# Hybrid RWKV-7 / pooling decoder block on one core: the SBUF addresses of the up and down projections' tiles, by order and padding

## The chip, the cores and the metric

The kernel is one program on one core of a Trainium2 chip. The metric is the device time of that core in microseconds (us). Before the change it is 2218.88 us, the median of three runs from 2218.65 to 2220.52.

## What is computed

The block is a decoder layer for one sequence of 512 tokens and 2048 channels in float32: an input projection, an RWKV-7 mixer beside a pooling mixer, an output projection, and a gated MLP with a depthwise convolution of width 3 between up projection and activation. Only the MLP matters here:

```python
def _conv_ffn(h, w_up, conv_w, conv_b, w_down):
    u = h @ w_up                         # 512 x 2048 @ 2048 x 11264
    up = jnp.pad(u, ((0, 0), (CONV_WIDTH - 1, 0), (0, 0)))
    y = conv_b
    for j in range(CONV_WIDTH):
        y = y + conv_w[j] * up[:, j:j + T]
    val, gate = jnp.split(y, 2, axis=-1)
    return (jax.nn.silu(gate) * val) @ w_down   # 512 x 5632 @ 5632 x 2048
```

`D_FF` is 5632, which is 44 tiles of 128 columns for the value and 44 for the gate.

## The kernel before

**How a float32 product is made.** Every operand is split into a high part (a copy rounded to the matmul's number format) and a low part (the rest). `mm3` (lines 129 to 133) makes one product of three matmuls: high weights with high activations (line 131), high weights with low activations (132), low weights with high activations (133). Each matmul record in the profile has a weight load (PEld) beside it: the weights are loaded anew for each of the three. `mm2` (1126 to 1128) does the same work in two matmuls where the activations are only 256 columns wide: the high weights with both parts side by side (512 columns, 1127) and the low weights with the high part (256 columns, 1128).

**The weight split.** `wsplit` (1272 to 1284) takes 128 x 1024 raw weights that a DMA has brought. ScalarE copies the high part (tile `uhi`, line 1279), VectorE subtracts for the low part (tile `ulo`, line 1283). Three pairs of buffers take turns: call 0, 3, 6, ... uses `whi0`/`wlo0` and call 1, 4, 7, ... uses `whi1`/`wlo1`, both in the pool `ea`; call 2, 5, 8, ... uses `whi2`/`wlo2` in the pool `ub`.

**The up projection** (about 824 to 1716 us of the profiled execution) is a blocked (Strassen-like) product: seven products of half size for each of the 44 pairs of a value tile and a gate tile. A **product** (`product`, 1286 to 1292) is one `wsplit` and 8 x 3 = 24 matmuls with 256 moving columns into one PSUM bank. There are 44 x 7 = 308 products, 7392 matmuls. I number them from 0 in their order on TensorE; number n uses weight pair n mod 3. Products 0 to 19 come from `first_two`, which makes the first two of the seven for the first ten pairs while the normalised activations of the second half of the tokens are still being made (`combos`). Product 20 is the first one of the main loop (1420 to 1477); product 22 is the first one on a `t` tile. In the main loop a pair in the later part has this order: `Y11` (tiles y0, y1), then the last product of the pair before on `T4` (t40, t41), then `Y21` (y2, y3), `T1` (t10, t11), `T2` (t20, t21), `Y22` (y220, y221), `T3` (t30, t31). Each of these activation tiles is 128 x 2 x 4 x 256 float32, high and low part, 8192 bytes in each partition. The profile leaves out the digits of tile names, so it writes `y` for Y11, Y21 and Y22, and `t` for T1 to T4. The last pair's products are numbers 300 to 306, and 307 is the last one on T4, which is made among the first products of the down projection.

**The down projection** (to the end) has 16 output tiles, and its 44 input tiles `act` are halved into h = 0 and h = 1. Each output tile and half takes three `wsplit` calls, for 8, 8 and 6 input tiles (`down`, 1499 to 1511): blocks of 24, 24 and 18 matmuls of 512 columns with `mm3`. In `down_half`, which makes the last eight output tiles for each half of the tokens, the blocks have 16, 16 and 12 matmuls of `mm2`. The `act` tiles are put into the up projection's places when these are done with (`ATAGS`, 1382): first y0 to y3, then t10, t11, t20, t21, y220, y221, t30, t31, t40.

**Order of work.** The compiler's scheduler sets the order of the instructions on each engine from their dependencies and from when buffers come free. The weight loads of the main loop are issued from SyncE's queue (`r1`, `w11`, `w12`, `w22`, `r3`) and two accumulating ones from GpSimd's.

**Where the tiles lie.** A pool puts its tiles one behind the other in the order in which their tags are first asked for. Pools on the left side follow each other from low addresses, and a pool on the right side ends at byte 229,344 of each partition. Worked out from the order and the sizes in the code, the byte addresses before are:

| tiles | pool | address mod 512 |
|---|---|---|
| y0 to y3 (Y11, Y21) | rb | 192 |
| t40 / t41 (T4) | ea | 224 / 352 |
| t1., t2., t3., y22. (T1, T2, T3, Y22) | ub | 480 |
| whi0, wlo0, whi1, wlo1 | ea | 256 |
| whi2, wlo2 | ub | 384 |
| the output projection's activations and split weights (earlier stage) | act, wts | 384 and 384 |

A slice for one matmul begins at a multiple of 512 bytes from the start of its weight tile and at a multiple of 1024 bytes from the start of its activation tile, so the class mod 512 holds for all slices of a tile. I write 192/256 for activations at 192 and weights at 256.

Small tiles that nothing reads set these classes: `edge` (32 bytes, lines 1274 to 1275) ahead of `whi0` in `ea` and of `whi2` in `ub`, and `edge2` (96 bytes, 1281 to 1282). The tile `ncw` (528 bytes, line 1358) is the last one of the pool `rb` and holds the negated convolution weights of the gate; `finish_pair` (1369) reads it. `rdiag` (1024 bytes, line 175) is a tile of the same pool that each of the RMS normalisations uses shortly.

Of the kernel before, what the change touches and what calls it, by code (L numbers as in the profile page):

```python
# [9 lines left out]
F32 = mybir.dt.float32  # L10
# [6 lines left out]
P = 128  # L17
T = 512
D = 2048
KT = D // P  # L20
NF = 44
# [6 lines left out]
NSLOT = 10  # L28
# [37 lines left out]
def block_kernel(ctx, tc, a, out, stop=None, dbg=None):  # L66
# [1046 lines left out]
    rb = ctx.enter_context(tc.tile_pool(name="rb", bufs=1, reuse_waits="tile"))  # L1113
# [3 lines left out]
    QW = 4 * P  # L1117
# [17 lines left out]
    def quad(i, name, dt=F32):  # L1135
        return rb.tile([P, 4, T], dt, tag=f"x2_{i}", name=name)
# [38 lines left out]
    for k0 in range(4, KT, 4):  # L1175
# [4 lines left out]
        for f in range(8):  # L1180
            out_block(f, k0)
            if k0 == 8 and f % 2:
                t = quad(f // 2, "x2")
# [10 lines left out]
    def out_half(hf, f):  # L1194
        ps = bank()
        acts = half([pairs[k] for k in range(KT)], hf)
        for k0 in range(0, KT, 4):
            wh, wl = split_weights(load_weights(a["wout"][f, :, k0 * P : k0 * P + WC]))
            for kk in range(4):
                sl = slice(kk * P, (kk + 1) * P)  # L1200
                mm2(ps, wh[:, sl], wl[:, sl], acts[k0 + kk], k0 + kk == 0, k0 + kk == KT - 1)
        out_done(f, [ps[:, 0:HT], ps[:, HT:T]], hf * HT, (hf + 1) * HT)
# [28 lines left out]
    for f in range(8, KT):  # L1231
# [7 lines left out]
                next(steps, None)  # L1239
        out_half(1, f)  # L1240

    ea = ctx.enter_context(tc.tile_pool(name="ea", bufs=1, reuse_waits="tile"))
    hctx.close()
    if stop == "B":
        return
# [6 lines left out]


    ub = ctx.enter_context(tc.tile_pool(name="ub", bufs=1, side="right", reuse_waits="tile"))
    free += [(ub, f"s{i}") for i in range(NSLOT)]

    class Slot:
# [12 lines left out]
    nsplit, lo_of = [0], [None]  # L1270

    def wsplit(src):
        n = src.shape[-1]
        if nsplit[0] in (0, 2):
            (ea, None, ub)[nsplit[0]].tile([P, 8], F32, tag="edge", name="edge")
        pool, tag = ((ea, "0"), (ea, "1"), (ub, "2"))[nsplit[0] % 3]
        nsplit[0] += 1
        hi = pool.tile([P, 2 * QW], F32R, tag="whi" + tag, name="uhi")
        S.copy(hi[:, 0:n], src)  # L1279
        lo = pool.tile([P, 2 * QW], F32R, tag="wlo" + tag, name="ulo")  # L1280
        if nsplit[0] in (2, 3):
            pool.tile([P, 24], F32, tag="edge2", name="edge2")
        lo_of[0] = V.tensor_tensor(lo[:, 0:n], src, hi[:, 0:n].bitcast(F32), op=ALU.subtract)  # L1283
        return hi, lo

    def product(ps, w, Y, start=True):
        wh, wl = wsplit(w)
        for k in range(8):
            sl = slice(k * P, (k + 1) * P)
            y = Y[k // 4]  # L1290
            mm3(ps, wh[:, sl], wl[:, sl], y[:, 0, k % 4, :], y[:, 1, k % 4, :], start=start and k == 0,
                stop=k == 7, more=not start)
# [62 lines left out]
        T4[g] = split4(ea, f"t4{g}", t4[g])  # L1355
    free.append((rb, "acc"))

    ncw = rb.tile([P, 3, NF], F32, tag="ncw", name="ncw")
    V.tensor_scalar(ncw, vec[:, COLS["cw"] : COLS["cw"] + 264].rearrange("p (i g j) -> p i g j", i=3, g=2)[:, :, 1, :],
                    -1.0, None, op0=ALU.mult)  # L1360

# [137 lines left out]
    def down(ps, f, h, acts, blocks=(0, 8, 16)):  # L1499
        for k0 in blocks:  # L1500
            n = min(8, NJ - k0)
            w = down_row()
            nc.sync.dma_start(w[:, 0 : n * P], a["wdn"][f, :, (h * NJ + k0) * P : (h * NJ + k0 + n) * P])
            wh, wl = wsplit(w[:, 0 : n * P])
            for k in range(n):
                sl = slice(k * P, (k + 1) * P)
                x = acts[k0 + k]
                if x.shape[-1] == HT:
                    mm2(ps, wh[:, sl], wl[:, sl], x, k0 + k == 0, k0 + k == NJ - 1)
                else:  # L1510
                    mm3(ps, wh[:, sl], wl[:, sl], x[:, 0, :], x[:, 1, :], start=k0 + k == 0, stop=k0 + k == NJ - 1)
# [73 lines left out]
    for f in range(NWF, KT):  # L1585
        n = f - NWF
# [107 lines left out]
```

## Time and profile before

| | us |
|---|---|
| median of three runs | 2218.88 |
| the profiled execution's own time | 2222.13 |
| its span, first to last instruction | 2220.4 |
| TensorE busy | 2157.1 (97%) |
| TensorE weight loads busy | 1890.5 (85%) |
| VectorE busy | 1617.1 (73%) |
| ScalarE busy | 1019.3 (46%) |
| GpSimd busy | 218.0 (10%) |
| mean granted TensorE clock | 0.994 |

A busy time is the union of an engine's records, and a matmul's record is longer than the distance from its start to the next one's start, because matmuls overlap. The pace of TensorE is therefore read from the start times in the timeline: the start of one product to the start of the next, divided by its number of matmuls.

### The profile page before, as it was taken

Reading aid. Unit: us, or ns where it says so; the run is one execution under the profiler, and the core shown is the slowest. Engines: PE = TensorE matmul, PEld = TensorE weight load, DVE = VectorE, ACT = ScalarE, POOL = GpSimd, SP = SyncE. Lnnn points to the kernel's source line nnn. Section 1 sums busy time; section 2 is a strip of 40 time slices with the busy share of each in tenths; the row PEclk is TensorE's granted clock in tenths of the full one; section 3 lists DMA queues with packets and bytes.
Section 4 is the critical chain, followed back from the end, with each engine's and each line's share of the span. In section 5 each row is a group of like instructions: output and inputs, shape, how many; then the busy total and the mean of one; then the engine's idle time right before and its main releaser. Section 6 shows DMA issues by size and latency. Waiting matters only on the chain.

```text
span 2220.4 us, 42522 instructions
## 1 busy us (share of the span) xinstructions
PE 2157.1 (97%) x17060; PEld 1890.5 (85%) x17060; DVE 1617.1 (73%) x2546; ACT 1019.3 (46%) x1465; POOL 218.0 (10%) x352
## 2 busy tenths in 40 slices
PE   6899999999999999999999999999999999999997
PEld 3677777777778889999999999999999888888886
DVE  7998898888853778888888877777777355253464
ACT  4354444444343466555555555555556322233453
POOL 0002111111100101101100000000000000110000
PEclk9999999999999999999999999999999999999998
DMA  9966665666447667988888777777777577564464
GB/s 392 379 207 201 198 200 172 194 185 189 119 132 253 204 174 252 249 249 243 230 242 247 209 200 197 198 204 203 200 194 240 158 287 252 194 206 117 137 194 144
DMA packets 169992, 468.65 MB, mean 211 GB/s; under 512 B 21361, under 2 KB 29505, under 8 KB 161729
## 3 DMA queue, kind: packets, MB, share of 16 engines
q1 hardware_dynamic: 128866, 364.45, 49.5%
q0 software_dynamic: 24752, 72.91, 15.6%
q10 hardware_dynamic: 16176, 28.58, 4.5%
q8 instruction: 134, 2.20, 0.4%
q14 instruction: 64, 0.52, 0.1%
HBM read 433.86 MB, written 31.99 MB: 210 GB/s over the span
## 4 chain that ended last, share of the span: by engine, by line
PE 85%; DVE 8%; DMA 3%; issue 2%; ACT 2%; POOL 0%; DVEq 0%; SPq 0%; ACTq 0%; POOLq 0%
PE b L131 18%; PE b L132 18%; PE b L133 18%; PE mm L555 11%; PE b L1127 5%; PE b L1128 3%; DVE wa L289 3%; DMA wrow<-wup 1%; DMA wraw<-win 1%; PE pb L957 1%; DVE war L674 1%; DVE wlo L328 1%; PE pa L621 0%; PE pb L997 0%; POOL x L797 0%
## 5 line engine op out<-in xcount | busy, mean ns | idle before, releaser
L132 PE MATMUL b<-t,uhi 128*128 128x256 f32 x1408 | 396.2, 281 | 0.0
L131 PE MATMUL b<-t,uhi 128*128 128x256 f32 x1408 | 396.0, 281 | 0.0
L133 PE MATMUL b<-t,ulo 128*128 128x256 f32 x1408 | 395.4, 281 | 0.0
L131 PE MATMUL b<-y,uhi 128*128 128x256 f32 x1056 | 296.0, 280 | 4.0 <-ACT uhi L1279 4.0
L133 PE MATMUL b<-y,ulo 128*128 128x256 f32 x1056 | 294.5, 279 | 0.7 <-DVE ulo L1283 0.7
L132 PE MATMUL b<-y,uhi 128*128 128x256 f32 x1056 | 295.0, 279 | 0.0
L555 PE MATMUL mm<-ahl,whi 128*128 128x512 f32 x864 | 290.8, 410 | 2.0 <-DVE rk L458 1.4
L1283 DVE TENSOR_TENSOR ulo<-wd,uhi 128x1024 fp32r<-128x1024 f32 (+1 forms) x120 | 136.0, 1134 | 205.7 <-ACT uhi L1279 201.1
L133 PEld LDWEIGHTS b<-t,ulo 128*128 128x128 f32 x1408 | 266.0, 189 | 0.0
L132 PEld LDWEIGHTS b<-t,uhi 128*128 128x128 f32 x1408 | 265.0, 188 | 0.0
L131 PEld LDWEIGHTS b<-t,uhi 128*128 128x128 f32 x1408 | 264.7, 188 | 0.0
L1279 ACT CAST uhi<-wquart 128x1024 fp32r<-128x1024 f32 x156 | 163.9, 1051 | 200.0 <-PE b L132 174.8
L1279 ACT CAST uhi<-wd 128x1024 fp32r<-128x1024 f32 (+1 forms) x120 | 117.2, 978 | 280.9 <-PE b L132 230.2
L1283 DVE TENSOR_TENSOR ulo<-wquart,uhi 128x1024 fp32r<-128x1024 f32 x156 | 190.9, 1224 | 65.2 <-ACT uhi L1279 65.0
L1279 ACT CAST uhi<-r 128x1024 fp32r<-128x1024 f32 x132 | 138.7, 1051 | 155.7 <-PE b L132 155.7
L132 PE MATMUL b<-act,uhi 128*128 128x512 f32 x528 | 208.5, 395 | 0.0
L131 PE MATMUL b<-act,uhi 128*128 128x512 f32 x528 | 208.5, 395 | 0.0
L133 PE MATMUL b<-act,ulo 128*128 128x512 f32 x528 | 207.8, 394 | 0.0
L1283 DVE TENSOR_TENSOR ulo<-r,uhi 128x1024 fp32r<-128x1024 f32 x132 | 161.3, 1222 | 60.9 <-ACT uhi L1279 60.9
L131 PEld LDWEIGHTS b<-y,uhi 128*128 128x128 f32 x1056 | 199.1, 189 | 4.5 <-ACT uhi L1279 4.4
L133 PEld LDWEIGHTS b<-y,ulo 128*128 128x128 f32 x1056 | 199.5, 189 | 1.0 <-DVE ulo L1283 0.9
L132 PEld LDWEIGHTS b<-y,uhi 128*128 128x128 f32 x1056 | 199.2, 189 | 0.1
(312 smaller groups left out, 4294.8 us busy)
## 6 DMA issues: line engine op xcount, KB each, us to landing
wquart<-wup SPq DMA_DIRECT2D x176, 512.0 KB, 4.7
wa<-ada SPq DMA_DIRECT2D x48, 1024.0 KB, 7.0
war<-ada SPq DMA_DIRECT2D x192, 256.0 KB, 4.1
wd<-wdn SPq DMA_DIRECT2D x80, 512.0 KB, 4.1
wraw<-win ACTq DMA_DIRECT2D x105, 256.0 KB, 4.2
wraw<-wout SPq DMA_DIRECT2D x96, 256.0 KB, 3.6
wquart<-wup POOLq DMA_DIRECT2D x44, 512.0 KB, 7.0
r<-wup SPq DMA_DIRECT2D x44, 512.0 KB, 4.5
```

Source lines behind the costliest of these rows:

```text
L131: PE.matmul(ps, wh, xh, start=start, stop=False, skip_group_check=more)
L132: PE.matmul(ps, wh, xl, start=False, stop=False, skip_group_check=more)
L133: return PE.matmul(ps, wl, xh, start=False, stop=stop, skip_group_check=more)
L289: V.scalar_tensor_tensor(wa[n], wa[n], 1.0, cb, op0=ALU.mult, op1=ALU.mult, accum_out=mod[:, j : j + 1])
L328: V.tensor_tensor(lo, raws[n], hi[:, :].bitcast(F32), op=ALU.subtract)
L555: PE.matmul(ps, w[:, sl], x, start=first, stop=k == KT - 1 and i == 2)
L674: V.scalar_tensor_tensor(wa, wa, 1.0, cqs[kq], op0=ALU.mult, op1=ALU.mult, accum_out=modq[:, kq, j : j + 1])
L957: PE.matmul(pt[HS[e], h, c * 2 * L : (c + 1) * 2 * L], nt[HS[e], s, :], rw[HS[e], s, :, :], start=True, stop=True)
L1127: PE.matmul(ps[:, :].rearrange("p (a b) -> p a b", a=2), wh, x, start=start, stop=False)
L1128: PE.matmul(ps[:, 0:HT], wl, x[:, 0, :], start=False, stop=stop)
L1279: S.copy(hi[:, 0:n], src)
L1283: lo_of[0] = V.tensor_tensor(lo[:, 0:n], src, hi[:, 0:n].bitcast(F32), op=ALU.subtract)
```

## The change

The change alters the order in which tags are first asked for, and the padding. A helper `lay` asks for a tile of each tag in a given order as soon as a pool is open; nothing reads or writes these tiles. In `ea` the order becomes t40, t41, 64 bytes of padding, then the weight pairs 0 and 1. In `ub` it becomes the ten slots, the eight activation tiles, 64 bytes, `whi2`, `wlo2`, and 224 bytes at the end. `ncw` loses its own place in `rb` and uses that of `rdiag`; `ea` begins where `ncw` began. The calls for `edge` and `edge2` in `wsplit` go. No instruction is added or removed.

```diff
+    def lay(pool, sizes):
+        for tag, n in sizes:
+            pool.tile([P, n], F32, tag=tag, name="lay")
+
     ea = ctx.enter_context(tc.tile_pool(name="ea", bufs=1, reuse_waits="tile"))
+    lay(ea, [("t40", 4 * T), ("t41", 4 * T), ("edge", 16)])
     hctx.close()
...
     ub = ctx.enter_context(tc.tile_pool(name="ub", bufs=1, side="right", reuse_waits="tile"))
+    lay(ub, [(f"s{i}", T) for i in range(NSLOT)])
+    lay(ub, [(f"{t}{g}", 4 * T) for g in range(2) for t in ("t1", "t2", "t3", "y22")])
+    lay(ub, [("edge", 16), ("whi2", 2 * QW), ("wlo2", 2 * QW), ("edge2", 56)])
...
     def wsplit(src):
         n = src.shape[-1]
-        if nsplit[0] in (0, 2):
-            (ea, None, ub)[nsplit[0]].tile([P, 8], F32, tag="edge", name="edge")
         pool, tag = ((ea, "0"), (ea, "1"), (ub, "2"))[nsplit[0] % 3]
...
-        if nsplit[0] in (2, 3):
-            pool.tile([P, 24], F32, tag="edge2", name="edge2")
...
-    ncw = rb.tile([P, 3, NF], F32, tag="ncw", name="ncw")
+    ncw = rb.tile([P, 3, NF], F32, tag="rdiag", name="ncw")
```

Worked out from the new order: `ea` begins at 101,568 (192 mod 512), t40 and t41 lie at 192, the weight pairs 0 and 1 at 256. `ub` is 94,496 bytes, begins at 134,848 (192 mod 512), its slots and its eight activation tiles lie at 192, and `whi2`, `wlo2` at 256. So all products have 192/256. The place of `whi2` and `wlo2` (220,928 to 229,120) is one that the output projection's split weights had; before, it was one that its activations had.

## The prediction

> **What bounds the kernel now.** I read the page's chain first, then the groups of the up projection's main loop, then the windows by stage, and last the timeline of TensorE alone, for its start times. The page's chain, by engine and by line:
>
> ```profile
> PE 85%; DVE 8%; DMA 3%; issue 2%; ACT 2%; POOL 0%; DVEq 0%; SPq 0%; ACTq 0%; POOLq 0%
> PE b L131 18%; PE b L132 18%; PE b L133 18%; PE mm L555 11%; PE b L1127 5%; PE b L1128 3%; DVE wa L289 3%; DMA wrow<-wup 1%; DMA wraw<-win 1%; PE pb L957 1%; DVE war L674 1%; DVE wlo L328 1%; PE pa L621 0%; PE pb L997 0%; POOL x L797 0%
> ```
>
> More than half of the span hangs on the three matmuls of `mm3`. The next rows are groups between 900 and 1704 us (behind the bar: busy time, mean ns of one, then idle time before them with what ended it), and then windows with busy time and count for TensorE, its weight loads, VectorE, ScalarE and GpSimd, and the granted clock, the DMA share and GB/s:
>
> ```profile
> L132 PE MATMUL b<-t,uhi 128*128 128x256 f32 x1392 | 391.7, 281 | 0.0
> L1283 DVE TENSOR_TENSOR ulo<-wquart,uhi 128x1024 fp32r<-128x1024 f32 x152 | 186.1, 1224 | 65.2 <-ACT uhi L1279 65.0
> L1279 ACT CAST uhi<-wquart 128x1024 fp32r<-128x1024 f32 x152 | 159.7, 1051 | 196.5 <-PE b L132 171.3 <-issue 24.9
> ```
>
> ```profile
> core 0: us, PE busy (x) PEld busy (x) DVE busy (x) ACT busy (x) POOL busy (x), PEclk, DMA share, GB/s
> 885.00:900.00 15.00, 15.00 (x134) 15.00 (x134) 15.00 (x15) 8.66 (x11) 3.49 (x5) 1.00 0.96 272
> 900.00:1100.00 200.00, 200.00 (x1695) 200.00 (x1694) 166.20 (x199) 107.99 (x135) 20.96 (x24) 1.00 0.87 245
> 1720.00:2078.00 358.00, 358.00 (x1542) 289.39 (x1541) 156.26 (x165) 104.61 (x132) 26.15 (x48) 1.00 0.59 194
> 2078.00:2220.00 142.00, 127.44 (x719) 110.28 (x717) 80.93 (x109) 64.49 (x84) 3.13 (x2) 0.95 0.59 172
> ```
>
> TensorE never idles here; VectorE waits for ScalarE's high parts, and ScalarE waits for TensorE to give a weight buffer back. So the weights are split ahead of need, and the stage lasts as long as its matmuls follow each other. Only their pace can shorten it.
>
> That pace isn't the same everywhere. First rows of product 17 and of product 22, with five whole products on y0 and y2 between them:
>
> ```profile
> 886.88 0.28 PE L131 MATMUL b<-y,uhi 128*128 128x256 f32 x1
> ...
> 900.48 0.28 PE L131 MATMUL b<-t,uhi 128*128 128x256 f32 x1
> ```
>
> 13.60 us over 120 matmuls is 113.3 ns each. Now the first rows of products 300 to 306, the last pair in the order that the section on the kernel gives:
>
> ```profile
> 1687.62 0.29 PE L131 MATMUL b<-y,uhi 128*128 128x256 f32 x1
> ...
> 1690.37 0.28 PE L131 MATMUL b<-t,uhi 128*128 128x256 f32 x1
> ...
> 1693.21 0.29 PE L131 MATMUL b<-y,uhi 128*128 128x256 f32 x1
> ...
> 1696.04 0.28 PE L131 MATMUL b<-t,uhi 128*128 128x256 f32 x1
> ...
> 1698.88 0.28 PE L131 MATMUL b<-t,uhi 128*128 128x256 f32 x1
> ...
> 1701.72 0.28 PE L131 MATMUL b<-y,uhi 128*128 128x256 f32 x1
> ...
> 1704.59 0.28 PE L131 MATMUL b<-t,uhi 128*128 128x256 f32 x1
> ```
>
> Per matmul (the distance divided by 24), with the classes of the table of addresses: Y11 at 192/256 takes 114.6 ns, T4 at 224 and 352/256 118.3, Y21 at 192/384 117.9, T1 at 480/256 118.3, T2 at 480/256 118.3, Y22 at 480/384 119.6. Shape, engine load and order of instructions are the same in all of them; the addresses differ. The one product at 192/256 is the fast one, and it is the class that all products get. The reader is to see that the 5 x 44 = 220 products on T1 to T4 and Y22, and the third of the y products that has pair 2, run below a pace that this same kernel already reaches, at full clock, in the window from 885 us.
>
> **The change part by part.** *Up projection.* The rows of products 22 and 306 span 284 products, 6816 matmuls: 1704.59 - 900.48 = 804.11 us, 117.97 ns each. At 113.33 ns they take 772.5 us: **-31.6 us**. Products 306 and 307 follow with 48 matmuls at some 5 ns less: **-0.2**. Products 0 to 21 I cost at nothing: most are on y tiles already, and their length is set by stalls of the norm between them.
>
> The saving lies on TensorE's own path, so nothing hides it. What comes late next is the split: per product VectorE's 1.22 us and ScalarE's 1.05 us, against a product of 2.72 us. VectorE's share goes from 166.20/200 = 83% to 87%, the DMA share from 0.87 to 0.91. Both stay under what the row from 885 us shows (VectorE 100%, DMA 0.96) with TensorE full.
>
> A rule of the Trainium skill speaks against all of this. "SBUF — State Buffer", section "Who interferes with whom", gives TensorE two independent read ports, one for the moving operand and one for the weights, and has it wait on nobody. By it the distance of two addresses costs nothing and this term is 0 instead of -31.6. The six products above disagree with it, 114.6 against 118.3 to 119.6 ns, unless their pace has a cause that only goes along with the addresses; that is the second rival.
>
> *Down projection.* The first rows of the second and third block (y0 to y3 with pairs 0 and 1, 192/256), and of three later blocks (y0 to y3 with pair 2, 192/384; then 480/256, 24 matmuls and the start of the 18):
>
> ```profile
> 1716.04 0.39 PE L131 MATMUL b<-act,uhi 128*128 128x512 f32 x1
> ...
> 1721.64 0.39 PE L131 MATMUL b<-act,uhi 128*128 128x512 f32 x1
> ...
> 1772.04 0.39 PE L131 MATMUL b<-act,uhi 128*128 128x512 f32 x1
> ...
> 1777.54 0.40 PE L131 MATMUL b<-act,uhi 128*128 128x512 f32 x1
> ...
> 1783.13 0.40 PE L131 MATMUL b<-act,uhi 128*128 128x512 f32 x1
> ```
>
> With 512 columns the order turns round: 192/256 takes 5.60/24 = 233.3 ns, 192/384 5.50/24 = 229.2, 480/256 5.59/24 = 232.9. The 192/384 blocks come 12 times in the first half (output tiles 4 to 15), 288 matmuls, and lose 4.1 ns each: 1.2 us. Seven blocks of the second half have that class in half of their matmuls: 84 x 4.1 = 0.3. Sum **+1.5**. Whether 192/256 everywhere holds 233.3 no row shows; its other end is that all 1584 matmuls run at the best 229.2 (1296 x 4.1 = 5.3 us gained). I take +1.5, the rows of the very class. The `mm2` blocks:
>
> ```profile
> 2104.55 0.40 PE L1127 MATMUL b<-act,uhi 128*128 128x512 f32 x1
> ...
> 2107.35 0.40 PE L1127 MATMUL b<-act,uhi 128*128 128x512 f32 x1
> ...
> 2109.48 0.39 PE L1127 MATMUL b<-act,uhi 128*128 128x512 f32 x1
> ```
>
> 16 matmuls, half of them at 192/256, take 175.0 ns each; 12 at 480/256 take 177.5. At most 16 x 12 x 2.5 ns = 0.5 us is there to gain; I take 0.
>
> *The new place of pair 2.* It overlaps weights of the output projection, so the third split has to wait for that projection's last matmul:
>
> ```profile
> 829.50 1.03 ACT L1279 CAST uhi<-wrow 128x1024 fp32r<-128x1024 f32 x1
> ...
> 832.16 0.28 PE L1128 MATMUL b<-ahl,wlo 128*128 128x256 f32 x1
> ...
> 837.65 0.37 PE L131 MATMUL b<-y,uhi 128*128 128x256 f32 x1
> ```
>
> The copy starts 2.9 us later, at 832.4, and with VectorE's 1.22 us the pair is ready at 834.7. Product 2, which needs it, starts at 837.65: cost 0, under cover of products 0 and 1; 2.9 us if that cover goes. Behind the copy on ScalarE stands nothing that starts before 833.5.
>
> *`ncw` in the place of `rdiag`.* Before, it is made long ahead; after, it waits until the second norm's TensorE broadcast has read `rdiag`:
>
> ```profile
> L1359 DVE TENSOR_SCALAR ncw<-vec x1: 284/284/284, 665.8 to 665.8; 128x132 f32<-128x132 f32 x1
> ```
>
> ```profile
> 843.28 0.59 PE L181 MATMUL b<-rdiag,cmat 128*128 128x256 f32 x2
> ```
>
> Its 0.28 us fall into the stretch up to 900 us, where VectorE is the full engine (15.00 of 15.00): **+0.3**. No load is moved past a queue, and the padding itself issues nothing.
>
> Sum: -31.6 - 0.2 + 1.5 + 0.3 = **-30.0 us**. The profiled execution, 2222.13 us (span 2220.4), would take 2192.1. It lies 3.25 us above the median, so the median goes from 2218.88 to **2188.9**.
>
> **The rivals.** *First: the slow rhythm returns in part.* Addresses are not all: the five fast products above hold two with pair 2 (192/384), the class that takes 117.9 ns in product 302. And product 4, at 192/256, runs slowly behind a stall:
>
> ```profile
> 843.83 0.28 PE L132 MATMUL b<-y,uhi 128*128 128x256 f32 x1
> ...
> 846.54 0.28 PE L131 MATMUL b<-y,uhi 128*128 128x256 f32 x1
> ```
>
> 2.71/23 = 117.8 ns. So there seem to be two rhythms, and a disturbance can choose between them. Against a long stay in the slow one speaks product 300, which comes behind a slow product and still averages 114.6. If a third of the loop stays slow, a third of 31.6 is lost: 2199.4.
>
> *Second: no gain.* The rhythm is set by the order of work and kept; everything runs at 117.8 as product 4 did. Saved: 6816 x 0.17 = 1.2 us, against +1.8 elsewhere: 2219.5.
>
> *Third: loads or VectorE take over* in the first twenty turns of the loop (its first 200 us show a DMA share of 0.87). These hold 10 x 7 + 10 x 5 = 120 products; if they keep their pace, 120/284 of 31.6 = 13.4 us are lost: 2202.3. Against it, SyncE's queue waits for free buffers (total, times, longest), so loads have time to spare:
>
> ```profile
> SPq L1430 <- DVE ulo L1283: 102.1, 43, 2.5
> ```
>
> *Fourth, the other side: the denser stream lowers the granted clock* in the whole loop. The last stage shows 0.95. At 113.33/117.97 = 0.96 the gain is gone; at 0.94 a matmul takes 120.6 ns, 6816 x 2.6 = 17.7 us more: about 2238. Against it, the window from 885 us is at this density with a clock of 1.00, and the 0.95 stands where TensorE idles 15 of 142 us.
>
> **How the numbers follow.** Forecast 0.77, the first rival 0.09, the second 0.06, the third 0.05, the fourth 0.03. The forecast's own range goes from 2182 (all of the down projection at its best pace) to 2192 (the third split uncovered). Upwards I reach to the first rival's 2199, and leave out the rest. A measurement tells about 0.2% (4.4 us) from no change, so faster is 0.77 + 0.09 + 0.05 = 0.91, same 0.06, slower 0.03.
>
> **What would show it.** Right: starts 113.3 to 113.5 ns apart in t products as in y products, on every third product too; about 772 us from product 22 to product 306; down blocks of 24 in 5.60 us, those of 1772 us as well; a granted clock of 1.00; no wait of TensorE in the loop. Wrong: t products at 117.8 (the second rival), fast and slow stretches by turns (the first), waits for `uhi` or `ulo` (the third).

## The result, and the profile after

The changed kernel takes 2191.57 us (median of 20 runs), the kernel before 2220.62 us (median of 20 runs beside them). The ratio is 0.9874, 95% interval 0.9859 to 0.9889: some 28 us are saved. The profiled execution took 2191.8 us, with a span of 2190.0 us and a mean granted clock of 0.994. Two of the 20 times, 2219.40 and 2223.24, stand 26 us and more above the other eighteen (2189.1 to 2193.3) at the same granted clock (0.995, where the eighteen have 0.993 to 0.997), and the ratio is one of mean times without the higher of the two; no profile of such an execution was taken, and the experiments show a mechanism of that size.

The chain of the changed kernel, by engine and by line, from its page:

```profile
PE 76%; issue 11%; DVE 8%; DMA 3%; ACT 2%; POOL 1%; POOLq 0%; DVEq 0%; SPq 0%; ACTq 0%
PE b L131 16%; PE b L133 16%; PE b L132 16%; PE mm L555 12%; DVE wa L289 3%; PE b L1127 2%; PE b L1128 1%; PE pb L957 1%; DMA al<-ad 1%; DMA wrow<-wup 1%; DVE ulo L1287 1%; DMA x<-dx 0%; PE pa L621 0%; DVE wlo L328 0%; DVE h L313 0%
```

The three matmuls still carry the end, with 16% each in place of 18%. (The 11% of "issue" is time for which this view found no releaser; TensorE is busy there, as the windows show.) The groups between 900 and 1672 us, and windows as before:

```profile
L132 PE MATMUL b<-t,uhi 128*128 128x256 f32 x1391 | 383.9, 276 | 0.0
L1287 DVE TENSOR_TENSOR ulo<-wquart,uhi 128x1024 fp32r<-128x1024 f32 x152 | 185.5, 1221 | 51.2 <-ACT uhi L1285 51.1
L1285 ACT CAST uhi<-wquart 128x1024 fp32r<-128x1024 f32 x152 | 159.7, 1051 | 173.8 <-PE b L132 149.5 <-ACT yv L1367 22.9
```

```profile
core 0: us, PE busy (x) PEld busy (x) DVE busy (x) ACT busy (x) POOL busy (x), PEclk, DMA share, GB/s
885.00:900.00 15.00, 14.34 (x123) 14.15 (x124) 14.79 (x16) 9.06 (x12) 2.96 (x4) 1.00 0.98 276
900.00:1100.00 200.00, 199.86 (x1764) 199.69 (x1763) 172.45 (x208) 112.18 (x142) 21.89 (x25) 1.00 0.89 252
1690.00:2048.00 358.00, 357.69 (x1533) 287.92 (x1532) 155.66 (x164) 103.43 (x130) 26.24 (x48) 1.00 0.58 192
2048.00:2190.00 142.00, 127.17 (x719) 109.93 (x718) 80.91 (x109) 64.53 (x84) 3.14 (x2) 0.96 0.59 172
```

VectorE still waits for ScalarE's high parts (51.1 us in place of 65.0) and ScalarE for TensorE (149.5 in place of 171.3), so the weights are still split ahead of need. The 200 us from 900 us hold 1764 matmuls where they held 1695, at the same clock. The starts of product 22, of products 300 to 303, and of product 306:

```profile
899.44 0.28 PE L131 MATMUL b<-t,uhi 128*128 128x256 f32 x1
...
1656.00 0.28 PE L131 MATMUL b<-y,uhi 128*128 128x256 f32 x1
...
1658.72 0.28 PE L131 MATMUL b<-t,uhi 128*128 128x256 f32 x1
...
1661.44 0.28 PE L131 MATMUL b<-y,uhi 128*128 128x256 f32 x1
...
1664.16 0.28 PE L131 MATMUL b<-t,uhi 128*128 128x256 f32 x1
...
1672.80 0.39 PE L131 MATMUL b<-t,uhi 128*128 128x256 f32 x1 [0.32 <-ACT cap L1464]
```

The loop takes 773.36 us in place of 804.11. Each of the three products between takes 2.72 us, 113.3 ns per matmul, on y and t tiles alike and with every pair of weights; before they took 114.6, 118.3 and 117.9. Product 306 waited 0.32 us, not for weights but for a copy that reads its PSUM bank (`cap`). The first rows of three blocks in the down projection (output tile 4; the first of them is the class that was quick before):

```profile
1740.53 0.40 PE L131 MATMUL b<-act,uhi 128*128 128x512 f32 x1
...
1746.13 0.40 PE L131 MATMUL b<-act,uhi 128*128 128x512 f32 x1
...
1751.73 0.40 PE L131 MATMUL b<-act,uhi 128*128 128x512 f32 x1
```

Both distances are 5.60 us, 233.3 ns per matmul. Between the two profiled executions the balance is: before product 22 -1.0 us (900.48 to 899.44), the loop -30.75, from product 306 to the end +1.45 (515.77 to 517.22): -30.3.

That leaves one thing of the early products, still in the changed kernel, all at 192/256. The starts of products 5 to 7, and of 8 to 10:

```profile
847.88 0.28 PE L131 MATMUL b<-y,uhi 128*128 128x256 f32 x1
...
850.70 0.28 PE L131 MATMUL b<-y,uhi 128*128 128x256 f32 x1
...
853.53 0.28 PE L131 MATMUL b<-y,uhi 128*128 128x256 f32 x1
...
856.32 0.28 PE L131 MATMUL b<-y,uhi 128*128 128x256 f32 x1
...
859.04 0.28 PE L131 MATMUL b<-y,uhi 128*128 128x256 f32 x1
...
861.76 0.28 PE L131 MATMUL b<-y,uhi 128*128 128x256 f32 x1
```

Products 5 and 6 run at 2.82 and 2.83 us, 117.7 ns; product 7 is disturbed; products 8 and 9 run at 2.72 us. The same classes of addresses and the same shapes have two rhythms, that is, two steady distances from start to start. So the addresses can't be the whole story.

### The profile page after: what moved, and what is told of

It reads as the page before. It is cut to its first block, busy times and chain, and to the rows that moved or that the text cites. A ratio compares the mean times of both kernels' runs of the same rounds, so it can differ in the third digit from the quotient of the medians.

```text
span 2190.0 us, 42524 instructions
## 1 busy us (share of the span) xinstructions
PE 2127.7 (97%) x17060; PEld 1858.0 (85%) x17060; DVE 1613.4 (74%) x2546; ACT 1018.5 (47%) x1465; POOL 218.5 (10%) x352
## 4 chain that ended last, share of the span: by engine, by line
PE 76%; issue 11%; DVE 8%; DMA 3%; ACT 2%; POOL 1%; POOLq 0%; DVEq 0%; SPq 0%; ACTq 0%
PE b L131 16%; PE b L133 16%; PE b L132 16%; PE mm L555 12%; DVE wa L289 3%; PE b L1127 2%; PE b L1128 1%; PE pb L957 1%; DMA al<-ad 1%; DMA wrow<-wup 1%; DVE ulo L1287 1%; DMA x<-dx 0%; PE pa L621 0%; DVE wlo L328 0%; DVE h L313 0%
## 5 line engine op out<-in xcount | busy, mean ns | idle before, releaser
L131 PE MATMUL b<-t,uhi 128*128 128x256 f32 x1408 | 388.8, 276 | 0.5 <-ACT cap L1464 0.3
L132 PE MATMUL b<-t,uhi 128*128 128x256 f32 x1408 | 388.6, 276 | 0.0
L133 PE MATMUL b<-t,ulo 128*128 128x256 f32 x1408 | 388.6, 276 | 0.0
L131 PE MATMUL b<-y,uhi 128*128 128x256 f32 x1056 | 292.2, 277 | 1.2 <-ACT uhi L1285 1.2
L132 PE MATMUL b<-y,uhi 128*128 128x256 f32 x1056 | 291.8, 276 | 0.0
L1287 DVE TENSOR_TENSOR ulo<-wquart,uhi 128x1024 fp32r<-128x1024 f32 x156 | 190.3, 1221 | 51.2 <-ACT uhi L1285 51.1
```

The costliest lines, as they stand in the source:

```text
L131: PE.matmul(ps, wh, xh, start=start, stop=False, skip_group_check=more)
L132: PE.matmul(ps, wh, xl, start=False, stop=False, skip_group_check=more)
L133: return PE.matmul(ps, wl, xh, start=False, stop=stop, skip_group_check=more)
```

## The experiments

**Which distance?** Three theories: A, only weights 64 bytes behind the activations let the 113.3 ns rhythm hold; B, any multiple of 64 bytes does; C, it is enough that all products have one class. Four kernels keep everything of the change (order, `ncw`, activations at 192) and set only the padding, so that the weights lie at distance 0, 32, 128 and 192. The edit for 192 (the others have 0, 8 or 32 in place of 48, and 72, 64 or 40 in place of 24; a pad of 0 is left out):

```diff
-    lay(ea, [("t40", 4 * T), ("t41", 4 * T), ("edge", 16)])
+    lay(ea, [("t40", 4 * T), ("t41", 4 * T), ("edge", 48)])
-    lay(ub, [("edge", 16), ("whi2", 2 * QW), ("wlo2", 2 * QW), ("edge2", 56)])
+    lay(ub, [("edge", 48), ("whi2", 2 * QW), ("wlo2", 2 * QW), ("edge2", 24)])
```

> The changed kernel with all activations at 192 as they are, and all split weights at 192 as well (distance 0 in place of 64), by the padding alone. Theory A (the distance of 64 bytes is what lets the 113.3 ns rhythm hold): the loop from product 22 to product 306 runs at 117.8 to 120 ns, some 803 to 818 us in place of 773.4, and the time is 2220 to 2236 us. Theory B (any multiple of 64 bytes does): 113.4 ns, about 2191. Theory C (what counts is that all products have one class, whichever, so that nothing throws the rhythm out): 113.4 ns, about 2191.

> The same with all split weights at 224 (distance 32). A and B: no fast rhythm, 118 to 120 ns per matmul (T4 at 224/256 and 352/384, which have this distance, showed 118.3 before), 2220 to 2236 us. C: 113.4 ns, about 2191.

> The same with all split weights at 320 (distance 128). A: 117.8 to 120 ns, 2220 to 2236 us. B and C: 113.4 ns, about 2191.

> The same with all split weights at 384 (distance 192, the class of Y11 and Y21 with pair 2 before, which showed 113.3 ns in products 17 and 20 and 117.9 in product 302). A in its strict form: 117.8 ns or a change between both, 2195 to 2222 us. A modulo 128, B and C: 113.4 ns, about 2191. In the down projection the blocks of 512 columns at 192/384 took 229.2 to 229.6 ns before; if that holds for all of them, the down projection gains 1584 x 3.9 = 6 us against the changed kernel.

Measured, one run each (the row for 64 is the median from above). The pace of the loop is the distance from product 22 to product 306 over 6816; the pace of the blocks with 512 columns is their mean distance in the down projection:

| distance | time, us | loop, ns per matmul | 512 columns, ns per matmul |
|---|---|---|---|
| 0 | 2228.59 | 120.0 | 226.7 |
| 32 | 2226.48 | 118.3 | 233.3 |
| 64 (the changed kernel) | 2191.57 | 113.5 | 233.3 |
| 128 | 2226.21 | 118.7 | 232.4 |
| 192 | 2213.72 | 117.8 | 228.9 |

The loop and two blocks of the down projection (24 matmuls to the next start) at distance 0, and the loop at distance 192:

```profile
902.63 0.28 PE L131 MATMUL b<-t,uhi 128*128 128x256 f32 x1
...
1720.55 0.28 PE L131 MATMUL b<-t,uhi 128*128 128x256 f32 x1
...
1786.19 0.39 PE L131 MATMUL b<-act,uhi 128*128 128x512 f32 x1
...
1791.63 0.39 PE L131 MATMUL b<-act,uhi 128*128 128x512 f32 x1
```

```profile
899.66 0.28 PE L131 MATMUL b<-t,uhi 128*128 128x256 f32 x1
...
1702.43 0.28 PE L131 MATMUL b<-t,uhi 128*128 128x256 f32 x1
```

817.92 us at distance 0 and 802.77 at 192, against 773.36. B falls (distances 0, 128 and 192 are slow), and so does C (all of them are uniform). The new order and the place of `ncw` can't be what saves 28 us: four kernels that have both are between 6 us faster and 9 us slower than the kernel before (2219.62 beside them). At distances 0, 32, 128 and 192 none of the products, the early ones included, is quicker than the loop: the shortest take 2.88, 2.84, 2.84 and 2.83 us. Distance 0 was not foreseen in one respect: it is the worst for 256 columns and the best for 512, where a block takes 5.44 us in place of 5.60.

**Distance or place?** The same distance, 32 bytes further up:

```diff
+    rb.tile([P, 8], F32, tag="padr", name="lay")
     steps = first_half()
...
-    lay(ub, [("edge", 16), ("whi2", 2 * QW), ("wlo2", 2 * QW), ("edge2", 56)])
+    lay(ub, [("edge", 16), ("whi2", 2 * QW), ("wlo2", 2 * QW), ("edge2", 48)])
```

(the tag stands in `rb` ahead of y0 to y3 and moves all that follows)

> The changed kernel with 32 bytes of padding ahead of y0 and the rest moved along: all activations at 224, all split weights at 288, distance 64 as before. If the distance alone counts: 113.4 ns, 773 us from product 22 to 306, about 2191.5. If the absolute place of 192/256 counts: 117.8 to 120 ns and 2220 to 2230.

Measured, one run: 2191.65 us. Products 22 and 306:

```profile
899.53 0.28 PE L131 MATMUL b<-t,uhi 128*128 128x256 f32 x1
...
1672.01 0.28 PE L131 MATMUL b<-t,uhi 128*128 128x256 f32 x1
```

772.48 us, 113.33 ns in the loop, without a single slow product. The distance counts; 192 and 256 themselves don't.

**One pair alone.** Only the third pair of weights moved away:

```diff
-    lay(ub, [("edge", 16), ("whi2", 2 * QW), ("wlo2", 2 * QW), ("edge2", 56)])
+    lay(ub, [("edge", 48), ("whi2", 2 * QW), ("wlo2", 2 * QW), ("edge2", 24)])
```

> The changed kernel with only the third pair of split weights moved by padding: whi2 and wlo2 at 384 (distance 192, which ran at 117.8 ns throughout when all pairs had it), pairs 0 and 1 at 256 as they are. If each product takes the pace of its own class: every third product 117.8 ns and the others 113.3 to 114.6, some 115 ns on the mean, 784 us from product 22 to 306, and about 2201 us. Rival, a rhythm once thrown out stays out: all products at 117.8 ns, 803 us, about 2220. Rival, two of three pairs are enough: 773 us, about 2191.

Measured, one run: 2192.38 us. Products 22, 31 to 34 and 306 (32 is on the third pair):

```profile
901.69 0.28 PE L131 MATMUL b<-t,uhi 128*128 128x256 f32 x1
...
926.17 0.28 PE L131 MATMUL b<-y,uhi 128*128 128x256 f32 x1
...
929.59 0.35 PE L131 MATMUL b<-t,uhi 128*128 128x256 f32 x1 [0.39 <-ACT uhi L1285]
...
932.49 0.28 PE L131 MATMUL b<-y,uhi 128*128 128x256 f32 x1
...
935.21 0.28 PE L131 MATMUL b<-t,uhi 128*128 128x256 f32 x1
...
1675.39 0.39 PE L131 MATMUL b<-t,uhi 128*128 128x256 f32 x1 [0.18 <-ACT cap L1464]
```

773.7 us, 113.5 ns in the loop, and apart from product 32, behind the stall, the products on the third pair take 113.3 ns as well, the class that ran at 117.8 when it was alone. The last rival holds: two of three pairs are enough. So with 256 columns a class doesn't have one pace; distances 64 and 192 each ran in two rhythms. With 512 columns it is otherwise: in the first half of this run's down projection the blocks on the third pair take 229.2 ns per matmul and the others 232.9 to 233.5 (the first block, which product 307 interrupts, left out), each close to the pace of its own distance in the table.

**Two rhythms?** One more matmul, into a bank that nobody reads, ahead of 34 products; its width grows by 8 columns with each turn of the loop and begins again at 8 after 256:

```diff
+    kick = [0]
+
     def product(ps, w, Y, start=True):
         wh, wl = wsplit(w)
+        if kick[0]:
+            PE.matmul(bank()[:, 0:kick[0]], wh[:, 0:P], Y[0][:, 0, 0, 0:kick[0]], start=True, stop=True)
+            kick[0] = 0
...
+            kick[0] = 8 * (n + 1) % 256 + 8
             product(pa, w11, Y11)
```

> The changed kernel, with one more matmul in each turn of the main loop that has ten or more as its pair (34 turns), ahead of the product of Y11, of 16 to 256 columns into a bank that nothing reads; the rest of the work is the same. It tests whether there are two rhythms at one and the same class that a disturbance chooses between. If so: behind some of these matmuls the products up to the next one run at 117.8 ns, behind others at 113.3, with nothing in between; the time is about 2195 plus 29.6 us times the slow share, 2195 to 2225. Rival, the slow products early in the stage come from their neighbours' work (norms, their loads): all products stay at 113.4 ns, about 2195.

Measured, one run: 2213.37 us, 116.8 ns on the mean. The starts of the first product of five turns in a row in this run (products 167, 174, 181, 188, 195), each behind an additional matmul:

```profile
1303.71 0.30 PE L131 MATMUL b<-y,uhi 128*128 128x256 f32 x1
...
1322.87 0.29 PE L131 MATMUL b<-y,uhi 128*128 128x256 f32 x1
...
1342.77 0.29 PE L131 MATMUL b<-y,uhi 128*128 128x256 f32 x1
...
1362.67 0.28 PE L131 MATMUL b<-y,uhi 128*128 128x256 f32 x1
...
1381.84 0.28 PE L131 MATMUL b<-y,uhi 128*128 128x256 f32 x1
```

A turn of 168 matmuls takes 19.16, 19.90, 19.90, 19.17 us, and 19.04 would be 168 x 113.3 ns. The slow turns are 0.74 us longer, 4.4 ns per matmul. Every turn behind such a matmul ran wholly at 113.3 or wholly at 117.8, once its first few matmuls were over; the rhythm stayed until the next one. That is the theory of two rhythms. The rival is out: the same products ran at 113.4 ns in the changed kernel and, behind some of these matmuls, at 117.8 ns here, with the same work around them.

**Both distances, by use.** The up projection gets distance 64 and the down projection distance 0, from the same buffers:

```diff
-NSLOT = 10
+NSLOT = 9
...
-    lay(ea, [("t40", 4 * T), ("t41", 4 * T), ("edge", 16)])
+    lay(ea, [("t40", 4 * T), ("t41", 4 * T), ("whi0", 2 * QW + 128), ("wlo0", 2 * QW + 128), ("whi1", 2 * QW + 16)])
-    lay(ub, [("edge", 16), ("whi2", 2 * QW), ("wlo2", 2 * QW), ("edge2", 56)])
+    lay(ub, [("wlo1", 2 * QW + 128), ("whi2", 2 * QW + 128), ("wlo2", 2 * QW + 16), ("edge2", 56)])
-    def wsplit(src):
+    def wsplit(src, at=16):
-        hi = pool.tile([P, 2 * QW], F32R, tag="whi" + tag, name="uhi")
+        hi = pool.tile([P, 2 * QW + 16], F32R, tag="whi" + tag, name="uhi")[:, at : at + 2 * QW]
-        lo = pool.tile([P, 2 * QW], F32R, tag="wlo" + tag, name="ulo")
+        lo = (ea if tag == "0" else ub).tile([P, 2 * QW + 16], F32R, tag="wlo" + tag, name="ulo")[:, at : at + 2 * QW]
...
-            wh, wl = wsplit(w[:, 0 : n * P])
+            wh, wl = wsplit(w[:, 0 : n * P], 0)
```

> Distance 64 for the up projection and distance 0 for the down projection: the tiles of the split weights lie at 192 and are 64 bytes longer, the up projection writes and reads them from byte 64 on, the down projection from byte 0 on; for the room, nine slots in place of ten, and wlo1 in the other pool. Up projection at 113.4 ns as in the changed kernel, down projection at 226.7 ns per matmul of 512 columns as with distance 0 everywhere (1584 x 6.6 = 10.5 us less) and about 1 us less in its last part: about 2180 us. If the pace of the down projection had another cause in that run than the distance, 2191. If nine slots are too few, TensorE waits in the loop and it is over 2191.

Measured: 2210.35 us (2206.76 to 2211.21, five runs), ratio to before 0.9946, 95% interval 0.9933 to 0.996. The forecast of 2180 us fell, and the profile says where. Products 31, 32 and 306 of this run:

```profile
924.10 0.28 PE L131 MATMUL b<-y,uhi 128*128 128x256 f32 x1
...
927.38 0.36 PE L131 MATMUL b<-t,uhi 128*128 128x256 f32 x1 [0.39 <-ACT uhi L1285]
...
1701.96 0.28 PE L131 MATMUL b<-t,uhi 128*128 128x256 f32 x1
```

Up to product 31 the loop runs at 113.3 ns. Product 32 waits for its weights for 0.39 us; from there to product 306 it is 774.58 us over 274 x 24 matmuls, 117.8 ns, to the end of the stage. The down projection gained as expected (226.7 ns). One stall of 0.4 us cost some 29 us, because nothing afterwards threw the slow rhythm out. Too few slots, the last branch of the forecast, don't explain it: this is TensorE's only wait in the loop, it is 0.39 us long, and the last experiment below has nine slots too. The changed kernel has a shorter stall at the same place (product 31 is 0.3 us longer than its neighbours), and came out of it fast.

**Does a mixture mend it?** In `pair2`, with ten slots, TensorE stalls there for 0.39 us too (its rows above: 3.42 us from product 31 to 32), and the rhythm was back one product later (2.90, then 2.72 us). The additional matmuls of `kick` on top of `pair2` (both edits above):

> The run pair2 (third pair of split weights at distance 192, the others at 64) with the same 34 additional matmuls as the run kick. There, with all pairs at 64, a rhythm that was thrown out stayed slow until the next additional matmul. Theory: a change of class from product to product pulls the rhythm back to the fast one, so here no more than some three products stay slow behind a disturbance, the loop from product 22 to 306 takes 777 to 784 us, and the time is about 2196 to 2203 us. Rival, the mixture does not matter and pair2 was merely never thrown out: as many slow products as in kick, about 796 us in the loop and 2213.

Measured, one run: 2198.21 us, loop 782.5 us. The starts of products 115 (behind an additional matmul) to 119:

```profile
1154.76 0.33 PE L131 MATMUL b<-y,uhi 128*128 128x256 f32 x1
...
1157.64 0.28 PE L131 MATMUL b<-t,uhi 128*128 128x256 f32 x1
...
1160.46 0.28 PE L131 MATMUL b<-y,uhi 128*128 128x256 f32 x1
...
1163.18 0.28 PE L131 MATMUL b<-t,uhi 128*128 128x256 f32 x1
...
1165.90 0.28 PE L131 MATMUL b<-t,uhi 128*128 128x256 f32 x1
```

2.88, 2.82, then 2.72 and 2.72 us: after two products the rhythm is back. In all 34 turns of the trace no more than three products in a row stayed slow behind the additional matmul, where `kick` had up to 35. The trace says more: a slow stretch always ended with the first product on the third pair, here product 116. One slow product followed where the additional matmul stood ahead of that pair (product 230), two ahead of pair 1 (223), three ahead of pair 0 (216). So it is the product at distance 192 among those at 64 behind which the fast rhythm is back; why is not shown. Last, this mixture in the kernel with both distances; only the up projection's third pair changes, to distance 192:

```diff
-    def wsplit(src, at=16):
+    def wsplit(src, at=None):
         n = src.shape[-1]
+        at = (16, 16, 48)[nsplit[0] % 3] if at is None else at
...
(the tiles of wsplit, whi1 and wlo2 are 48 longer in place of 16, edge2 is 24)
```

> The run both64_0 (up projection at distance 64, down projection at distance 0) with the up projection's third pair at distance 192, so that the rhythm mends itself if the theory of pair2kick holds: up projection at 113.5 ns, down projection at 226.7, about 2180 us. If the mixture does not matter, the disturbance at product 31 throws it out as in both64_0: about 2210.

Measured: 2183.93 us (2181.56 to 2186.22, five runs), ratio to before 0.9832, interval 0.9818 to 0.9847; it lies wholly below the changed kernel's 0.9859 to 0.9889. Products 22 and 306, and two blocks of the down projection:

```profile
900.51 0.28 PE L131 MATMUL b<-t,uhi 128*128 128x256 f32 x1
...
1676.53 0.39 PE L131 MATMUL b<-t,uhi 128*128 128x256 f32 x1 [0.64 <-ACT cap L1465]
...
1742.17 0.39 PE L131 MATMUL b<-act,uhi 128*128 128x512 f32 x1
...
1747.61 0.39 PE L131 MATMUL b<-act,uhi 128*128 128x512 f32 x1
```

776.02 us in the loop (113.9 ns) and 5.44 us a block. Products 31 and 32, with two stalls, take 3.73 and 2.90 us, and product 33 is back at 2.72; from product 31 on `both64_0` had 275 slow ones. Two more stalls, ahead of products 104 and 116, leave one slow product each (2.90 us). This version beats both kernels.

## Why the prediction was right, and where it was not

- *TensorE's pace sets the stage, and all products would take the pace of 192/256*: right in size; as a mechanism it is half of the matter. -30.75 us measured for -31.6; at 113.46 ns in place of 113.33. The 0.9 us between them are the stalls at products 31 and 305 and the slow product behind the first. But the pace doesn't belong to the class alone: the loop of `both64_0`, at the same distance, ran at 117.8 ns behind one stall. That the changed kernel came out of its own stall fast is luck as far as the runs show.
- *The split, the loads and VectorE keep up*: right. 172.45 of 200 us is 86% for VectorE and 0.89 for the DMA share, where 87% and 0.91 were worked out. "No wait of TensorE in the loop" held but for one wait for a high part ahead of product 32 and the one at 306; both are in the 0.9 us.
- *Down projection*: right. 5.60 us for the blocks that took 5.50; from product 306 to the end +1.45 us, where -0.2 + 1.5 = +1.3 was the sum. The other end that was left open, all matmuls at the best pace, exists at other distances only: 228.9 ns at 192 and 226.7 at 0.
- *The third split*: the wait came and was covered. Its copy:

```profile
833.71 1.05 ACT L1285 CAST uhi<-wrow 128x1024 fp32r<-128x1024 f32 x1 [2.60 <-PE b L1128]
```

  It waited for the output projection as told. Product 2 started 1.2 us later than before (838.88), but the copy into y3 that runs ahead of all this was already 1.24 us later (828.95 against 827.71), so this is no cost of the wait.
- *`ncw`*: it moved behind the norm, to 847.5 us, at 0.287 us:

```profile
L1363 DVE TENSOR_SCALAR ncw<-vec x1: 287/287/287, 847.5 to 847.5; 128x132 f32<-128x132 f32 x1
```

  From product 0 to product 22 it is 74.1 us in place of 76.6, so the +0.3 can't be seen; that products 0 to 21 would gain nothing was 2.4 us off. The stretch ahead of them was 1.4 us longer.
- *The sum*: -30.0 us forecast, -30.3 between the profiled executions, -29.05 between the medians of 20. That the first two agree so well is in part luck: the loop gave 0.9 us less than forecast, and the stretch ahead of product 22 gave 1.0 us where +0.3 was forecast. The measured time is 2.7 us above the forecast one, of which 1.7 lie in the kernel before, whose median moved from 2218.88 in three runs to 2220.62 in 20.
- *The first rival*, the slow rhythm, was the right thing to fear. It exists, and by `kick`'s slow turns the whole loop in it costs 4.4 ns x 6816 = 30 us. What I gave as evidence against a long stay, that product 300 came back within one product, was read wrongly: in the kernel before, classes change from product to product, and `pair2kick` shows that such a change can bring the fast rhythm back (that it did so for product 300 is argued, not tried). With distance 64 for all, as the change makes it, the slow rhythm didn't mend by itself in `both64_0` (274 products) nor behind the slow matmuls of `kick`. That the two high times of the changed kernel come from it is argued from their size (28 and 32 us above the median) and from their unchanged clock.
- *The granted clock* stayed at 1.00 through the loop; the fourth rival is out for this stage.
- *The rule of the Trainium skill* ("SBUF — State Buffer", "Who interferes with whom", TensorE's two read ports are independent) doesn't account for what was measured here: moving nothing but the weights' addresses by 64 bytes took the loop from 120.0 to 113.5 ns per matmul.

## What to carry to other kernels

Where matmuls and weight loads alternate back to back, look at start-to-start times per product, not at busy time, and compare them by the distance of weights and moving operand modulo 512 bytes. Find the distance for each width of the moving operand: of the five tried here, 64 was best for 256 columns and 0 for 512. And ask of a fast rhythm whether it comes back after a stall; one product at another distance among its like can bring it back. That `both_p2` is free of high times like the two of the changed kernel isn't shown, since it has five runs only.

## What the runs showed that I had not expected

- The same stream of matmuls at the same distance and clock has two steady rhythms, 113.3 and 117.8 ns. One extra matmul of 8 to 256 columns chose between them up to the next one, and a wait of 0.4 us for 274 products.
- Distance 192 alone stayed at 117.8 ns in the whole loop, but held 113.3 ns between products at distance 64 (`pair2`). Why is open. None of the products of `dist192`, not even those behind the early stalls, ran fast, and whether the class alone could stay fast was not tried.
- What in the hardware reads in this pattern stays open. Within a product the distances of the slices differ by multiples of 512 bytes, and all its matmuls keep one pace, so the distance counts modulo 512. It could be modulo 256 as well, but not modulo 128, since 64 and 192 differ (113.5 against 117.8 ns, and 233.3 against 228.9). The runs don't show which part of the chip is shared.
- In the second half of the down projection (512 and 256 columns by turns) the distance matters little: from its first matmul to its last it took 125.1 us in the changed kernel and 124.2 at distance 0.
